# A hybrid attention and ConvFFN layer on one core: spreading the later attention steps over the blocks by a table

## Chip, core and metric

One core of one Trainium2 chip runs the whole layer in a single launch. Times are device microseconds (us) of that core. The engines are TensorE (PE, with its weight loads as PEld), VectorE (DVE), ScalarE (ACT), GpSimd (POOL) and SyncE (SP, which here only issues DMAs).

## What is computed

One layer on a sequence of 2048 tokens of width 1024, all in float32:

```
h = rms_norm(x);  sb_q, sb_k, sb_v, g_q, g_k, g_v, g_lr, g_og = split(h @ w_in)
o_sb  = head_rms_norm(stick_breaking_attention(q, k, v))     # 8 heads of 64, strictly causal
o_gla = head_rms_norm(gla_chunked(...)) * silu(g_og)         # 4 heads, gated linear attention
x = x + concat(o_sb, o_gla) @ w_out
h = rms_norm(x)
a, val = split(causal_depthwise_conv(h @ w_ffn_up), 2)       # 2 x 2816 columns, 3 taps
x = x + (silu(a) * val) @ w_ffn_down
return rms_norm(x)
```

In stick-breaking attention the weight of key s for query t is beta_ts times the product of (1 - beta_tj) over s < j < t, with beta the sigmoid of the scaled score.

## The kernel before

Every float32 factor is split into a high part in float32r and a low part that holds the rest, and a product is three matmuls (high by high, high by low, low by high). The split is one copy on ACT (line 102 for weights, line 94 for results in PSUM) and one subtraction on POOL or DVE (lines 103 and 95).

The sequence is cut into four blocks of 512 tokens. First come the input projections, the gated linear attention, the output gate, and the stick-breaking attention of block 0 (the first 675 us). Then `ffn(b)` runs for the four blocks in turn. Each call has an output projection with w_out (`accumulate`, two halves of 512 columns), a norm with transposing matmuls (tpu), and three groups of 8, 7 and 7 chunks of the FFN. A group is an up stage (`ups`, per chunk two pieces of 24 matmuls) and a down-projection (`accumulate` again, tiles d and draw). In block 0 the weights come raw from DRAM: SP loads a chunk (uraw, draw, or wraw for the first half of w_out), ACT and POOL split it, POOL's queue writes the split pair to DRAM scratch (wup, wdn, wou). Blocks 1 to 3 load the split pairs.

The attention of blocks 1, 2 and 3 stands beside this as a second generator, `attention_steps`, `later` in the driver. Its units are (block i, head h, key block c), four steps each: 288 steps and 8 more to drain the pipeline, 296 in all. Step n makes the weights of its query tile (z on PE, two sigmoids on ACT, a scan, cy and a product on DVE; in a diagonal unit, c equal to i, POOL masks two tiles), transposes those of step n - 5 (tp on PE, ws on ACT and DVE), and multiplies those of step n - 6 with v (acc on PE). z lies in a pool of two PSUM banks. A finished head is normed and written to osc, from which the next block's output projection reads.

PE's instructions stand in the order in which the program is written; the other engines' and the queues' order is made by a scheduler from it. The driver fixes PE's order: `ffn` yields the estimated length of what it has just issued (2.6 after each half of an up piece of 24 matmuls or a chunk of a down-projection; 395.2 a block), the driver adds that to `clock`, and issues attention steps until their number has caught up:

```
for dt in ffn(b, oT, order if b == 0 else None, nextT):
    clock += dt
    while done < total and done < clock / SPAN * total:
        next(later, None)
        done += 1
```

`LEAD` steps (4) are made before the first block. `need` is asserted: block b + 1 finds its attention done. While `done < total`, a down-projection gathers in the four banks that it shares with the up stage, and later in four of attention's banks, with six more buffers for its weights (`after_attention`).

Of the kernel before, what the change touches and what calls it, by code (L numbers as in the profile page):

```python
# [21 lines left out]
NB = S // TB  # L22
# [11 lines left out]

LAG = 5

SPAN = 1030.0
FILL = 4.0

FIRST = 4 * SBH + LAG + 4  # L40
# [10 lines left out]
def hybrid_block_kernel(ctx, tc, x, attn_norm_g, w_in, w_gate_up, b_gate_up, sb_out_g,  # L51
# [66 lines left out]
    if True:  # L118
# [21 lines left out]
        for n in (6, 7, 8, 9, 10, 11, 14, 15, 0, 1, 2, 3, 4, 5, 12, 13):  # L140
            b, u = n // 4, n % 2
# [319 lines left out]
    class Ring:  # L461
# [3 lines left out]
        def next(self):  # L465
            self.n += 1
            return self.items[(self.n - 1) % len(self.items)]
# [487 lines left out]
    total = 4 * SBH * (2 + 3 + 4) + LAG + 3  # L955
    need = [0, 4 * SBH * 2 + LAG + 3, 4 * SBH * 5 + LAG + 3, total]
    done = 0
    clock = 0.0
    results = []
    order = (4, 5, 6, 7, 0, 1, 2, 3)  # L960
    oT = [oT.get(f) for f in order]
# [2 lines left out]
        done += 1  # L964
    for b in range(NB):
        nextT = []
        for dt in ffn(b, oT, order if b == 0 else None, nextT):
            clock += dt
            while done < total and done < clock / SPAN * total:
                next(later, None)  # L970
                done += 1
        assert b + 1 == NB or done >= need[b + 1]
        oT = nextT
# [27 lines left out]
```

## Time and profile before

| | |
|---|---|
| median of 3 runs | 2754.53 us (2751.18 to 2754.88) |
| the profiled execution | 2760.47 us, its span 2758.8 us |
| PE, PEld busy (share of the span) | 2694.3 us (98%), 2234.3 us (81%) |
| DVE, ACT, POOL busy | 1685.5 us (61%), 1147.0 us (42%), 611.6 us (22%) |
| chain that ended last | PE 86%, DVE 5%, DMA 4%, ACT 2% |
| granted clock of PE, mean | 0.996 |

The first instruction of the profile is time 0. In the profiled execution block 0's `ffn` runs from about 678 to 1265 us, block 1's to 1830, block 2's to 2336 and block 3's to 2751. The last attention step stands in block 2's second up stage. A wait is named by what PE was about to do and by the instruction that released it. An engine's busy time counts an instruction from its start to its end; PE's matmuls overlap.

### The profile page before, as it was taken

The page shows a single profiled execution, that of the slowest core. Times are in us where ns is not written, and L with a number is a line of the kernel's source. Part 1 is how long each engine was busy: PE and PEld are TensorE (multiplying, and loading weights), DVE is VectorE, ACT ScalarE, POOL GpSimd, SP SyncE. Part 2 cuts the span into 40 slices and gives each one's busy share as a digit, 9 for nine tenths or more (in the row PEclk, how much of TensorE's full clock was granted, in tenths as well). Part 3 has the DMA queues.
Part 4 walks back from the last instruction along what each step waited for, and adds up shares of the span by engine and source line. Part 5 has one row for each costly group of instructions (what it writes and reads, how often), then busy time and mean ns, then how long its engine had stood idle before and what let it go on. Part 6 is the DMA issues. An engine that isn't in the chain of part 4 may idle for free.

```text
span 2758.8 us, 36075 instructions
## 1 busy us (share of the span) xinstructions
PE 2694.3 (98%) x13004; PEld 2234.3 (81%) x13004; DVE 1685.5 (61%) x2778; ACT 1147.0 (42%) x2371; POOL 611.6 (22%) x937
## 2 busy tenths in 40 slices
PE   8999999999799999999999999999999999999998
PEld 7878888888688778887888888888888888888887
DVE  5246755467677687876776777777867334242333
ACT  5455533345465455554543444445434222220112
POOL 2001212215555556542111111111110000000000
PEclk9999999999999999999999999999999999999999
DMA  6214644467667677768455555574554656555552
GB/s 191 92 64 173 228 144 156 131 188 242 224 225 257 224 243 255 243 236 274 156 185 181 175 174 174 186 253 152 177 177 150 231 192 221 203 197 191 198 191 84
DMA packets 232169, 526.92 MB, mean 191 GB/s; under 512 B 32294, under 2 KB 120630, under 8 KB 209462
## 3 DMA queue, kind: packets, MB, share of 16 engines
q1 hardware_dynamic: 200742, 387.76, 42.3%
q0 software_dynamic: 31104, 136.33, 13.9%
q8 instruction: 102, 1.67, 0.3%
q14 instruction: 77, 0.63, 0.1%
q10 hardware_dynamic: 144, 0.52, 0.1%
HBM read 382.99 MB, written 141.56 MB: 190 GB/s over the span
## 4 chain that ended last, share of the span: by engine, by line
PE 86%; DVE 5%; DMA 4%; ACT 2%; issue 1%; POOL 1%; SPq 0%; ACTq 0%; POOLq 0%; DVEq 0%
PE ups L886 11%; PE ups L887 11%; PE ups L888 11%; PE d L765 7%; PE d L764 7%; PE d L766 7%; PE z L533 4%; PE tp L566 4%; PE mm L170 2%; PE mm L168 2%; PE mm L169 2%; PE acc L582 2%; PE mm L180 2%; PE mm L179 2%; PE mm L178 2%; PE acc L581 2%
## 5 line engine op out<-in xcount | busy, mean ns | idle before, releaser
L886 PE MATMUL ups<-h2h,u 128*128 128x512 f32 x1408 | 552.2, 392 | 3.9 <-DVE x L791 3.9
L887 PE MATMUL ups<-h2l,u 128*128 128x512 f32 x1408 | 551.1, 391 | 0.0
L888 PE MATMUL ups<-h2h,u 128*128 128x512 f32 x1408 | 550.3, 391 | 0.0
L886 PEld LDWEIGHTS ups<-h2h,u 128*128 128x128 f32 x1408 | 265.2, 188 | 60.6 <-DVE x L791 4.3
L95 DVE TENSOR_TENSOR ws<-tp,ws 128x512 fp32r<-128x512 f32 (+1 forms) x320 | 194.0, 606 | 193.2 <-ACT ws L94 192.3
L888 PEld LDWEIGHTS ups<-h2h,u 128*128 128x128 f32 x1408 | 265.0, 188 | 57.2
L887 PEld LDWEIGHTS ups<-h2l,u 128*128 128x128 f32 x1408 | 265.0, 188 | 55.4
L764 PE MATMUL d<-d,g 128*128 128x512 f32 x736 | 290.4, 395 | 3.8 <-ACT d L102 1.3
L94 ACT ACTIVATE ws<-tp 128x512 fp32r<-128x512 f32 (+1 forms) x320 | 170.3, 532 | 297.0 <-PE tp L566 292.8
L765 PE MATMUL d<-d,g 128*128 128x512 f32 x736 | 288.7, 392 | 1.2 <-POOL d L103 1.2
L766 PE MATMUL d<-d,g 128*128 128x512 f32 x736 | 288.4, 392 | 0.0
L898 DVE SCALAR_TENSOR_TENSOR ct<-ups,cwb,ct 128x511 f32<-128x511 f32 x176 | 131.7, 748 | 249.4 <-POOL ct L897 196.2
L893 ACT ACTIVATE ct<-ups,cwb 128x512 f32<-128x512 f32 x176 | 136.5, 775 | 340.0 <-PE ups L888 339.8
L549 DVE TENSOR_TENSOR_SCAN wtB<-mt,cy 128x512 f32<-128x512 f32 x192 | 249.0, 1297 | 4.4 <-ACT mt L538 4.3
L791 DVE TENSOR_TENSOR x<-d,x 128x512 f32<-128x512 f32 x128 | 85.8, 683 | 164.1 <-PE d L766 164.0
L897 POOL TENSOR_TENSOR ct<-ct,hadd 128x2 f32<-128x2 f32 x132 | 26.7, 202 | 688.5 <-ACT halo L895 324.3
L538 ACT ACTIVATE mt<-z 128x512 f32<-128x512 f32 (+2 forms) x320 | 170.6, 533 | 14.3 <-PE z L536 6.2
L764 PEld LDWEIGHTS d<-d,g 128*128 128x128 f32 x736 | 138.3, 188 | 35.3 <-DVE x L791 2.8
L765 PEld LDWEIGHTS d<-d,g 128*128 128x128 f32 x736 | 138.3, 188 | 31.2 <-POOL d L103 1.8
L766 PEld LDWEIGHTS d<-d,g 128*128 128x128 f32 x736 | 138.2, 188 | 30.8
L168 PE MATMUL mm<-hh,w 128*128 128x512 f32 x384 | 151.3, 394 | 0.0
L170 PE MATMUL mm<-hh,w 128*128 128x512 f32 x384 | 149.3, 392 | 0.9 <-POOL w L103 0.9
(265 smaller groups left out, 5374.2 us busy)
## 6 DMA issues: line engine op xcount, KB each, us to landing
u<-wup SPq DMA_DIRECT2D x132, 1024.0 KB, 4.7
d<-wdn SPq DMA_DIRECT2D x94, 512.0 KB, 3.5
wup<-u POOLq DMA_DIRECT2D x44, 1024.0 KB, 6.6
kvA<-kvs POOLq DMA_DIRECT2D x52, 512.0 KB, 4.6
uraw<-in_w_ffn_up_dram SPq DMA_DIRECT2D x44, 512.0 KB, 4.7
wdn<-d POOLq DMA_DIRECT2D x44, 512.0 KB, 4.9
d<-wou SPq DMA_DIRECT2D x38, 512.0 KB, 4.6
dw<-wdn SPq DMA_DIRECT2D x38, 512.0 KB, 4.3
```

Source lines behind the costliest of these rows:

```text
L94: nc.scalar.activation(hi, ps, AF.Copy)
L95: nc.vector.tensor_tensor(out=lo, in0=ps, in1=hi.bitcast(F32), op=ALU.subtract)
L168: nc.tensor.matmul(ps, whi[k][:, fs], hh[b][k // 4][:, k % 4, :], start=(k == 0), stop=False)
L170: nc.tensor.matmul(ps, wlo[k][:, fs], hh[b][k // 4][:, k % 4, :], start=False, stop=(k == KT - 1))
L538: nc.scalar.activation(m[:, lo:TB], z[:, :width], AF.Sigmoid, scale=-0.125)
L549: nc.vector.tensor_tensor_scan(out=pp[:, ::-1], data0=mr, data1=mr, initial=1.0 if prev is None else prev, op0=ALU.mult, op1=ALU.bypass)
L764: nc.tensor.matmul(accs[t], gh[:, ts], whi, start=(ci == 0), stop=False)
L765: nc.tensor.matmul(accs[t], gh[:, ts], wlo, start=False, stop=False)
L766: nc.tensor.matmul(accs[t], gw[:, ts], whi, start=False, stop=(ci == G - 1))
L886: nc.tensor.matmul(ps, whi[:, k, :], hk, start=(k == 0), stop=False)
L887: nc.tensor.matmul(ps, whi[:, k, :], lk, start=False, stop=False)
L888: nc.tensor.matmul(ps, wlo[:, k, :], hk, start=False, stop=(k == KT - 1))
```

## The change

The one rate for all blocks becomes a table with a number for each block, and the count starts anew at each block: in block b, `RATE[b]` steps per 395 units of its own clock, on top of those made before it. SPAN gave 296 / 1030 * 395 = 113.5 a block from the first unit on, with the four steps ahead counted in it. The last block has no steps in either.

```diff
-SPAN = 1030.0
+
+DENSE = 395.0
+RATE = (86, 130, 113)
...
-    clock = 0.0
...
         nextT = []
+        clock, begun = 0.0, done
         for dt in ffn(b, oT, order if b == 0 else None, nextT):
             clock += dt
-            while done < total and done < clock / SPAN * total:
+            while b + 1 < NB and done < total and done < begun + clock / DENSE * RATE[b]:
                 next(later, None)
                 done += 1
```

No instruction is added or removed; the order differs from the first output projection on. Line numbers of the changed kernel are two higher from there on. Three places:

PE, the first half of block 0's output projection (d is its PSUM tile, wsplit and wmore its split weights, z the scores of a step, tp the transposes of an earlier step). Before, its first step:

```order
L764 MATMUL d_6374<-wsplit,g_0_5527 128x512
L765 MATMUL d_6374<-wsplit,g_0_5527 128x512
L766 MATMUL d_6374<-wsplit,g_1_5528 128x512
L647 MATMUL tpo<-ident,ohp 128x128 x4
L533 MATMUL z<-kvA,qA 128x512 x2
L764 MATMUL d_6371<-wmore,g_0_5976 128x512
```

With the change, its first two steps:

```order
L768 MATMUL d_6373<-wsplit,g_1_5528 128x512
L535 MATMUL z<-kvA,qA 128x512 x2
L766 MATMUL d_6371<-wsplit,g_0_5527 128x512
...
L768 MATMUL d_6374<-wsplit,g_1_5528 128x512
L568 MATMUL tp<-ident,wtA 128x128 x4
L535 MATMUL z<-kvA,qA 128x512 x2
L766 MATMUL d_6371<-wmore,g_0_5976 128x512
```

The first step stood behind 72 matmuls of the projection and now stands behind nine; the second, with the first transposes, stood twelve matmuls later and now comes behind 24 in all.

ACT at the same place (mt and wt are a step's sigmoids, u the third weight of the up stage, d and wsplit and wmore weights of the output projection). Before:

```order
L102 ACTIVATE d_6310<-draw 128x512
L102 ACTIVATE wsplit<-wraw 128x512 x2
L538 ACTIVATE mt_5034<-z 128x384
L540 ACTIVATE wtA<-z 128x384
L538 ACTIVATE mt_5035<-z 128x512
L540 ACTIVATE wtA<-z 128x512
L102 ACTIVATE wmore<-wraw 128x512
L102 ACTIVATE u_6308<-uraw 128x1024
L102 ACTIVATE wmore<-wraw 128x512
```

With the change:

```order
L104 ACTIVATE d_6310<-draw 128x512
L540 ACTIVATE mt_5034<-z 128x384
L542 ACTIVATE wtA<-z 128x384
L540 ACTIVATE mt_5035<-z 128x512
L542 ACTIVATE wtA<-z 128x512
L104 ACTIVATE u_6308<-uraw 128x1024
L104 ACTIVATE wsplit<-wraw 128x512
L540 ACTIVATE mt_5034<-z 128x512
L542 ACTIVATE wtB<-z 128x512
L104 ACTIVATE wsplit<-wraw 128x512
L96 ACTIVATE ws_5042<-tp 128x512
```

The split of the up weight moved ahead of both wsplit and of the first ws; it was behind wsplit and ahead of one wmore.

ACT, near the end of block 0's first down-projection (d are splits of its weight chunks, ws copies of a step's transposed weights). Before:

```order
L102 ACTIVATE d_6310<-draw 128x512
L94 ACTIVATE ws_5042<-tp 128x512
L538 ACTIVATE mt_5035<-z 128x256
L540 ACTIVATE wtB<-z 128x256
L102 ACTIVATE d_6309<-draw 128x512 x2
L94 ACTIVATE ws_5043<-tp 128x512
```

With the change:

```order
L104 ACTIVATE d_6309<-draw 128x512
L104 ACTIVATE d_6310<-draw 128x512
L104 ACTIVATE d_6309<-draw 128x512
L96 ACTIVATE ws_5042<-tp 128x512
L540 ACTIVATE mt_5035<-z 128x256
L542 ACTIVATE wtC<-z 128x256
```

Three splits stand in a row where two did, as fewer steps lie between them.

## Rows read from the trace of the kernel before

**Rows 1.** Windows: stretch, length; busy PE, PEld, DVE, ACT, POOL; clock, DMA, GB/s:

```profile
678.00:1265.00 587.00, 558.17 (x2704) 459.92 (x2702) 430.49 (x649) 309.97 (x622) 323.34 (x379) 0.99 0.71 243
1265.00:1830.00 565.00, 560.79 (x2758) 465.70 (x2759) 413.35 (x668) 252.46 (x535) 87.21 (x187) 1.00 0.55 185
...
2636.00:2712.00 76.00, 76.00 (x337) 62.94 (x336) 33.52 (x47) 18.36 (x26) 2.56 (x13) 1.00 0.46 160
1675.00:1778.00 103.00, 103.00 (x499) 85.49 (x498) 83.14 (x132) 49.61 (x104) 16.06 (x33) 1.00 0.50 171
```

**Rows 2.** Waits of PE, 675 to 1265 us: us in total, times, longest:

```profile
PE acc L582 <- DVE ws L95: 6.4, 7, 2.1
PE d L764 <- ACT wmore L102: 5.5, 1, 5.5
PE ups L886 <- DVE x L791: 3.9, 1, 3.9
PE d L765 <- POOL wmore L103: 3.3, 1, 3.3
PE tpu L856 <- DVE dg L851: 2.5, 1, 2.5
PE d L764 <- ACT d L102: 1.3, 1, 1.3
PE d L764 <- DVE x L791: 1.3, 2, 0.8
PE d L765 <- POOL d L103: 1.2, 2, 0.9
PE d L764 <- DVE ct L900: 1.2, 1, 1.2
PE acc L581 <- ACT ws L94: 1.1, 2, 0.9
PE d L765 <- POOL wsplit L103: 0.8, 1, 0.8
PE z L533 <- ACT wtA L540: 0.8, 1, 0.8
```

**Rows 3.** Waits of PE, 1265 to 1830 us, those of attention:

```profile
PE acc L581 <- ACT ws L94: 1.0, 1, 1.0
...
PE acc L582 <- DVE ws L95: 0.9, 2, 0.7
```

**Rows 4.** Windows of the three half-clock stretches after 675 us, columns as in rows 1:

```profile
706.49:710.76 4.27, 4.27 (x12) 3.18 (x10) 0.00 (x0) 0.00 (x0) 0.41 (x1) 0.50 0.98 393
946.90:949.89 2.99, 2.99 (x8) 2.31 (x7) 2.48 (x4) 0.00 (x0) 1.61 (x2) 0.50 0.99 390
1022.08:1025.07 2.99, 2.99 (x9) 2.34 (x8) 2.30 (x5) 0.90 (x3) 0.84 (x3) 0.50 0.94 224
```

**Rows 5.** Timeline, first output projection: start, length, engine, instruction [idle before <-releaser]:

```profile
677.78 0.40 PE L764 MATMUL d<-wsplit,g 128*128 128x512 f32 x1
...
681.56 4.47 SPq L880 DMA_DIRECT2D uraw<-in_w_ffn_up_dram  x2
...
687.48 0.49 ACT L540 ACTIVATE wtA<-z 128x384 f32<-128x384 f32 x1
...
694.91 0.68 DVE L555 TENSOR_TENSOR wtA<-wtA,wtB 128x512 f32<-128x512 f32 x1
...
700.21 1.06 ACT L102 ACTIVATE u<-uraw 128x1024 fp32r<-128x1024 f32 x1 [8.62 <-DMA uraw<-in_w_ffn_up_dram]
```

**Rows 6.** Timeline, end of the first down-projection, ACT and PE:

```profile
943.07 0.63 ACT L102 ACTIVATE d<-draw 128x512 fp32r<-128x512 f32 x1 [4.65 <-DMA draw<-in_w_ffn_down_dram]
...
945.56 0.50 PE L886 MATMUL ups<-h2h,u 128*128 128x512 f32 x1 [3.88 <-DVE x L791]
```

**Rows 7.** Tile cy, block 0 then block 1: duration in ns, min/median/max:

```profile
L553 DVE TENSOR_TENSOR cy<-wtB,mt x65: 129/159/2061, 685.4 to 1260.1; 128x1 f32<-128x1 f32 x65
...
L553 DVE TENSOR_TENSOR cy<-wtB,mt x81: 142/159/163, 1272.5 to 1827.1; 128x1 f32<-128x1 f32 x81
```

## Prediction

> **What bounds it now.** I read first the windows by block [rows 1]. TensorE (PE) has an instruction in flight for 558 of block 0's 587 us, 561 of block 1's 565 and all of two pure stretches, so PE sets the pace everywhere, and what can be won is what PE loses. The difference between the blocks is in the other columns: POOL works 323 us in block 0, which splits weights, and 87 us in block 1, which reads them split; DVE works about the same in both.
>
> The share of PE busy time hides how full PE is. The Trainium skill, Perfetto Trace Analysis, section Identifying the Most-Contended Engine, says that matmul busy time is no good measure of headroom and LDWEIGHTS busy share is; the page of the profile has 81% there, which by that rule alone would leave 19%, some 520 us (an estimate from that page's rule). The trace sets the scale: in the last up stage, with no attention and no gap in PE, weight loads fill 62.94 of 76 us, 82.8%, and in block 1 465.70 of 565, 82.4%; a full PE reads so here [rows 1]. Block 0 has 459.92 of 587, 78.3%. At 82.4% its loads would take 558 us: some 29 us are lost in block 0, and almost nothing in block 1.
>
> The waits of PE say where [rows 2]: twelve kinds, 29.3 us, in block 0. Four things are mixed there. (a) The start of the first output projection, 5.5 + 3.3 + 0.8 for its weights and 0.8 for a z bank, 10.4 us. (b) Attention's own chain, acc on ws, 6.4 + 1.1 = 7.5 us. (c) Banks that come free late in the down-projections (3.9, 1.3, 1.2), and splits that come late there or in the output projection's second half (1.3, 1.2), 8.9 us. (d) The rstd chain, 2.5 us. On top, PE runs at 0.50 of its clock, the lower level of 1.2 GHz, over 4.27 + 2.99 + 2.99 us behind idle stretches; half of that, 5.1 us, is lost [rows 4]. Block 1 has only 1.9 us of waits on ws in 114 steps [rows 3].
>
> **What the change moves.** By the code's own clock (395.2 units per block) the three blocks run 110, 114 and 68 steps now, after the four ahead; with the table they run 87, 131 and 74. So 23 steps leave block 0, 17 go to block 1 and 6 to block 2. No instruction is added or taken away.
>
> A step's price on PE: the third up stage of block 1 is 103 us long and holds 21 steps, the same stage without steps 76 us [rows 1]; (103 - 76) / 21 = 1.29 us. So 23 x 1.29 = 29.7 us leave block 0 and come back as 21.9 + 7.7 us later. Where PE is full this sums to zero. A step's DMA issues (a key/value load on POOL's queue per four steps, a query load per head) and its write of the head's result on SP's queue move with it; POOL's and SP's queues in block 0 lose about six key/value loads and two or three result writes, and no wait of rows 2 is on one of them. Their worth is taken as zero: POOL is busy 55% of that block. So the answer lies in the waits.
>
> **Attention's waits in block 0, (b)**: 7.5 us, and the half-clock stretch at 1022 us behind one of them, 1.5 us: 9.0. With 24% fewer steps proportion alone takes off 2.2; if only close-packed steps collide, all 9.0 go. A step may come after every half of an up piece (12 matmuls); the up stages of block 0 go from three steps in four such halves to about one in two, but the diagonal units still wait on POOL behind weight splits. I take half, **-4.5** (ends -9 and +2, the upper one for the seven collisions of rows 2 falling otherwise).
>
> **Down-projections, (c)**: 8.9 us and the stretch at 946.9 us, 1.5: 10.4. The largest item is a chain on ACT: the split of a weight chunk waits 4.65 us for its DMA, the ws copy and the sum into x stand behind it, and PE's next bank is released 3.88 us late [rows 6]. The order rows show three splits in a row ahead of ws where there were two, so that this block is not gone for sure. PE also has less attention to fill with, while each chunk takes its DMA, ACT and POOL as before. Half of the 5.4 there, and 1.8 of the other 5.0, which are DVE's and the splits' queues: **-4.5** (ends -10.4 and +4, one more such wait).
>
> **The first output projection, (a)** is worked through, since the table starts its count at the four steps already made: five steps fall into the projection's first half, where there were two. PE starts at 677.78 and meets the fifth step's z after nine matmuls, at 679.9 [rows 5]. The z pool has two banks; the third z's sigmoids end at 688.0 (687.48 + 0.49), a wait of 8.1. Fifteen matmuls of 0.23 (76 / 337 in the pure stretch of rows 1) follow to 691.4; then the transposes need the fourth weight tile, done at 695.6 (694.91 + 0.68): 4.2. A z pair and 24 matmuls, 26 x 0.23, lead to 701.6. Now acc needs ws, which on ACT stands behind the split of the third up weight, whose load was issued at 681.56 and starts at 700.21 [rows 5]. Its 1.06, five more ACT operations of about 0.5 and one of 0.7 on DVE (the sigmoid and the product of the same rows) end near 704.5: 2.9. The waits are 15.2 against 10.4, but two steps more are done by then, 2.6: **+2** (ends -4 and +8; the load's landing alone can move it by the 4.65 that rows 6 show for a late one).
>
> The rstd wait and block 1's waits on x and on its first transposes are untouched.
>
> **Block 1** gets runs of five or six steps in consecutive half-pieces, where it had three. DVE per half-piece: 33.52 / 28 = 1.20 of dense work, and (83.14 - 33.52) / 21 = 2.36 a step, 3.56 in all; PE takes 76 / 28 + 1.29 = 4.0 [rows 1]. DVE still has 11% left inside a run. Its 1.9 us of waits on ws [rows 3] would be 2.2 in proportion; I take **+1** (ends 0 and +14, see the third rival). Block 2 keeps its rate, 113 a block, and runs some 25 units longer: the down-projection there still finds attention in its first half and keeps the shared banks, as all of block 1's do, which show no wait on them: 0.
>
> **Sum**: -4.5 - 4.5 + 2 + 1 = -6. The profiled execution took 2760.47 us (span 2758.8), so 2754.5 in its own terms; the median of the three runs is 2754.53, 5.9 below it, so **2748.5**.
>
> **Rivals.** 1. The collisions go altogether. POOL's work slows DVE: cy, a one-column product of 159 ns, takes up to 2061 ns in block 0 and at most 163 ns in block 1 [rows 7]. The Trainium skill, SBUF — State Buffer, section Who interferes with whom, says that the port pair of GpSimd and DVE is an exclusive lock for operations with two SBUF inputs, the second one blocking fully; rows 7 agree. As a mechanism here: every step moved takes its DVE products away from POOL's splits, so (b) and (c) both go, -9 - 10.4 + 2 + 1 = -16: 2738. Against it: only seven of 110 steps wait on DVE's ws now, at three steps in four half-pieces, so distance is not what makes most of them. 2. The weight chain takes it back: PE in block 0 has less of its own to do per chunk, and waits for chunks instead. (c) stays whole and (a) costs 8 in place of 2, -4.5 + 8 + 1 = +4.5, or with (a) at 2 -1.5: 2753 to 2759, say 2755. For it: rows 6 and the ACT order. Against: (c) is seven waits in all of block 0, so that the chain does not bind most chunks. 3. Slower: DVE becomes the bound in block 1's up stages. They hold 75 steps (66 now). Each pair of up pieces ends with a burst of DVE products, and a run of six leaves it less room to drain. If one step in four waits 0.9 us on ws, as one of block 0's does on average (6.4 / 7), that is 17 us: -6 + 17 - 1 = +10: 2764.5. It decides where DVE's time per half-piece passes PE's 4.0 us, 0.44 above my 3.56. Against it: now the same stages have 81% on DVE and next to no waits. 4. The change does not do what it says: excluded by the order rows, but its effect may be nil: 2754.5.
>
> **Chances.** Forecast 0.46, rival 1 0.16, rival 2 0.17, rival 3 0.17, rival 4 0.04. About 0.2% (5.5 us) is what a measurement of this kernel can tell from no change, so below 2749.0 is faster. Of the forecast's 0.46 the part beyond it is 0.27, as its sum lies just past the bound: faster 0.27 + 0.16 = 0.43; same 0.19 + 0.14 + 0.04 = 0.37; slower 0.03 + 0.17 = 0.20. The range runs from rival 1's centre less a microsecond to rival 3's centre, 2737 to 2765, and leaves out about half of each, 0.17. The forecast's own range is 2741 to 2756.
>
> **What would show it.** Block 0 should be 29.7 + 8 us shorter, near 549 us; its waits on ws near 3 to 4 us; its first stretch should show PE waiting for z and tp instead of wmore. Block 1 should be near 588 us with under 4 us of waits on ws. The forecast is wrong if block 1's ws waits pass 8 us (rival 3), or if block 0's down-projections wait as long as now (rival 2).

## Result and profile after

The changed kernel is slower. Its median is 2778.78 us (2762.35 to 2781.75, 7 runs) against 2754.88 (2751.18 to 2759.22, 7 runs) of the kernel before, a ratio of 1.0069 with a 95% interval of 1.0052 to 1.0087. Run unedited twice more, each time beside its own runs of the kernel before, it gave 1.0057 [1.0037, 1.0076] and 1.0056 [1.0040, 1.0072]. The forecast of 2748.5 was a gain where there is a loss, and the median lies outside the range of 2737 to 2765.

The first profile is of the execution with the lowest of the seven times (2762.35 us). A profile of another execution of the same program, label again, is of 2780.96 us and nearer to the median, so most rows below are from that one. First the windows by block, columns as in [rows 1], of the changed kernel's first profile:

```profile
677.80:1235.50 557.70, 532.24 (x2541) 439.25 (x2540) 385.80 (x563) 276.52 (x556) 311.27 (x354) 0.98 0.74 251
1235.50:1826.30 590.80, 585.50 (x2904) 485.68 (x2902) 454.52 (x745) 281.00 (x595) 100.10 (x209) 1.00 0.54 182
1826.30:2338.90 512.60, 507.83 (x2431) 420.39 (x2429) 313.81 (x495) 189.09 (x394) 50.14 (x125) 1.00 0.56 190
```

and of again:

```profile
678.60:1251.40 572.80, 537.42 (x2542) 441.83 (x2540) 387.75 (x563) 276.14 (x556) 312.80 (x354) 0.97 0.72 244
1251.40:1842.10 590.70, 585.42 (x2901) 485.63 (x2900) 454.55 (x745) 281.15 (x594) 100.40 (x209) 1.00 0.55 182
1842.10:2355.90 513.80, 509.54 (x2432) 421.81 (x2430) 313.52 (x494) 189.14 (x393) 49.90 (x125) 1.00 0.56 190
```

Cut at the same places (the first d matmul of each block), the kernel before has 591.70, 566.30 and 501.50 us; its block 0:

```profile
677.80:1269.50 591.70, 560.52 (x2720) 461.92 (x2719) 434.65 (x657) 313.01 (x631) 325.94 (x385) 0.99 0.72 244
```

So block 0 is shorter, as was meant, by 18.9 us in again and by 34.0 in the first profile, where 29.7 us of steps have left it; blocks 1 and 2 grow by 24.4 and 12.3 us in again and by 24.5 and 11.1 in the first profile. Blocks 1 and 2 are alike in the two executions to 1.2 us; what differs most from one execution to the next is block 0.

The loss is not idle time alone. Over the whole execution PE is busy 2705.4 us in again and 2694.3 before, with the same 13004 matmuls, at a mean granted clock of 0.992 and 0.996. So 11.1 of the 20.5 us between the two spans are PE running longer, about what the clock gives (an estimate: 0.004 of 2779 us is 11 us), and 9.4 are idle time of PE.

The waits of PE in block 0 of again (675 to 1251.4 us: us in total, times, longest), to be read against [rows 2]:

```profile
PE acc L584 <- DVE ws L97: 7.3, 7, 3.0
PE acc L583 <- ACT ws L96: 6.4, 4, 3.2
PE z L535 <- ACT wtA L542: 6.3, 2, 5.6
PE tpu L858 <- DVE dg L853: 4.8, 2, 3.2
PE d L766 <- ACT d L104: 3.2, 2, 2.8
PE tpo L649 <- DMA kvB<-osc: 2.4, 1, 2.4
PE d L767 <- POOL d L105: 2.2, 3, 0.9
PE d L766 <- DVE x L793: 1.5, 2, 1.2
PE tp L568 <- DVE wtA L557: 1.1, 2, 0.8
```

With one more of 0.9 they make 36.1 us, in a block with 23 steps fewer. Before, it is 32.1 us to the same cut: the 29.3 of [rows 2], which end at 1265 us, and two waits between there and 1269.5:

```profile
PE tpo L647 <- DMA kvB<-osc: 1.5, 1, 1.5
PE tpo L647 <- ACT wtC L540: 1.3, 1, 1.3
```

The waits for wmore (5.5 and 3.3) and the 3.9 on the second up stage's first bank are gone, as the prediction had it; waits on ws have gone up from 7.5 to 13.7, z's from 0.8 to 6.3, the rstd chain's (dg) from 2.5 to 4.8.

To place this, block 0 is cut into its seven stages, the first being the output projection with the tpu stage behind it. Lengths are those of windows; the steps are the sigmoids of tile mt counted in the same windows; the last column adds 1.29 us to the difference for each step that left, so that it holds the waits and what PE loses at its lower clock. Counting the moved work by PE's matmul records instead (27 us for 162 of them in [rows 1]) moves single stages by up to 1.6 us and changes no sign.

| stage | before, us (steps) | again, us (steps) | difference | without the steps |
|---|---|---|---|---|
| projection, tpu | 85.3 (13) | 96.3 (14) | +11.0 | +9.7 |
| up 1 | 116.4 (24) | 108.2 (18) | -8.2 | -0.5 |
| down 1 | 66.1 (12) | 61.0 (9) | -5.1 | -1.2 |
| up 2 | 110.3 (21) | 95.6 (15) | -14.7 | -7.0 |
| down 2 | 52.4 (10) | 52.1 (8) | -0.3 | +2.3 |
| up 3 | 103.5 (21) | 102.4 (16) | -1.1 | +5.4 |
| down 3 | 57.7 (11) | 57.2 (9) | -0.5 | +2.1 |
| block 0 | 591.7 (112) | 572.8 (89) | -18.9 | +10.8 |

Two things went wrong. The first output projection is 10 us longer, and what the three stages after it gain (8.7 us together) the last three stages, which had only 3.9 us of waits before, lose again (9.8 us).

### The profile page after: what moved, and what is told of

Read it like the earlier page. It is cut to its first block, busy times and chain, and to the rows that moved or that the text cites. A ratio compares the mean times of both kernels' runs of the same rounds, so it can differ in the third digit from the quotient of the medians.

```text
span 2760.6 us, 36068 instructions
## 1 busy us (share of the span) xinstructions
PE 2697.8 (98%) x13004; PEld 2237.7 (81%) x13004; DVE 1690.7 (61%) x2778; ACT 1145.7 (42%) x2371; POOL 611.2 (22%) x937
## 4 chain that ended last, share of the span: by engine, by line
PE 88%; DVE 5%; DMA 3%; ACT 2%; issue 1%; POOL 1%; SPq 0%; ACTq 0%; POOLq 0%; DVEq 0%
PE ups L888 11%; PE ups L889 11%; PE ups L890 11%; PE d L766 7%; PE d L767 7%; PE d L768 7%; PE z L535 4%; PE tp L568 4%; PE mm L172 2%; PE mm L170 2%; PE mm L171 2%; PE acc L584 2%; PE mm L181 2%; PE mm L182 2%; PE mm L180 2%; PE acc L583 2%
## 5 line engine op out<-in xcount | busy, mean ns | idle before, releaser
L766 PE MATMUL d<-d,g 128*128 128x512 f32 x748 | 296.4, 396 | 2.2 <-DVE x L793 1.2
L767 PE MATMUL d<-d,g 128*128 128x512 f32 x748 | 294.6, 394 | 1.7 <-POOL d L105 1.7
L768 PE MATMUL d<-d,g 128*128 128x512 f32 x748 | 294.1, 393 | 0.0
L766 PEld LDWEIGHTS d<-d,g 128*128 128x128 f32 x748 | 141.3, 189 | 34.4 <-DVE x L793 2.6
L767 PEld LDWEIGHTS d<-d,g 128*128 128x128 f32 x748 | 141.5, 189 | 32.2 <-POOL d L105 2.3
L768 PEld LDWEIGHTS d<-d,g 128*128 128x128 f32 x748 | 141.3, 189 | 31.6
L170 PE MATMUL mm<-hh,w 128*128 128x512 f32 x384 | 151.2, 394 | 0.0
L171 PE MATMUL mm<-hl,w 128*128 128x512 f32 x384 | 150.2, 391 | 0.0
```

The lines of the kernel that those rows point to most:

```text
L170: nc.tensor.matmul(ps, whi[k][:, fs], hh[b][k // 4][:, k % 4, :], start=(k == 0), stop=False)
L171: nc.tensor.matmul(ps, whi[k][:, fs], hl[b][k // 4][:, k % 4, :], start=False, stop=False)
L766: nc.tensor.matmul(accs[t], gh[:, ts], whi, start=(ci == 0), stop=False)
L767: nc.tensor.matmul(accs[t], gh[:, ts], wlo, start=False, stop=False)
L768: nc.tensor.matmul(accs[t], gw[:, ts], whi, start=False, stop=(ci == G - 1))
```

## Experiments

The theories at the start: A, that the early start of block 0's count, the steps in the first output projection, is the loss; B, that it is block 1's denser steps; C, that block 0's weights come late because there is less attention to cover them. Four runs share one set of runs of the kernel before (2757.79 us, 29 runs).

**again**: the changed kernel, no edit.

> The changed kernel once more, nothing edited, for a profile of a typical run: the one profile that exists (2762.35 us) is the fastest of seven runs whose median is 2778.78 us. All theories: a median of 2775 to 2780 us. Theory A (the start of block 0, where five steps now come early): the trace of a run near 2778 us has 10 us or more of additional PE waits and half-clock time before 765 us. Theory B (block 1's denser steps): the additional time is in block 1, as waits of acc on ws. Theory C (block 0's weights come late because it has less attention to cover them): it is in block 0's down-projections and up stages after 765 us.

Measured 2775.19 us (2764.11 to 2780.96, 6 runs), ratio 1.0057 [1.0037, 1.0076]. The loss is there a second time.

**late_start**: block 0 counts from 0 in place of the four steps made, with a rate that ends at the same 91.

```diff
-RATE = (86, 130, 113)
+RATE = (90, 130, 113)
+START = (0, None, None, None)
...
-        clock, begun = 0.0, done
+        clock, begun = 0.0, done if START[b] is None else START[b]
```

> The table, but block 0 counts the four steps ahead in it, as before the change: 90 per 395 units from nothing, so its first own step comes at 17.6 units and no longer at the first yield. Block 0 still ends with 91 steps made, blocks 1 and 2 as in the change. Theory A: near or below the kernel before, 2745 to 2758 us. Theories B and C: 2772 to 2780 us, as the change.

Measured 2758.36 us (2750.04 to 2770.77, 12 runs), ratio 1.0004 [0.9988, 1.0020]. It is 0.4 us above theory A's range and far from that of B and C. Nearly all of the loss is gone, with block 0 as thin and block 1 as dense as in the changed kernel. Its windows by block:

```profile
677.20:1231.40 554.20, 530.08 (x2542) 436.18 (x2541) 385.74 (x563) 276.91 (x556) 303.62 (x354) 0.99 0.74 252
1231.40:1823.70 592.30, 587.01 (x2902) 486.80 (x2900) 454.65 (x745) 281.15 (x594) 100.07 (x209) 1.00 0.55 182
1823.70:2338.00 514.30, 509.48 (x2432) 421.79 (x2430) 313.99 (x495) 189.24 (x394) 51.03 (x125) 1.00 0.56 190
```

Block 0 is 37.5 us shorter than before, 7.8 more than its steps, close to what the prediction had (29.7 + 8). Projection and tpu take 77.2 us with 10 steps, up 3 takes 98.0 with 17. But blocks 1 and 2 take 26.0 and 12.8 us more, where 23 steps at 1.29 us are 29.7: 9.1 us above that price, and nothing is won.

**early_start**: the old spread (114, 228 and 296 made at the ends), counted from the four steps made.

```diff
-RATE = (86, 130, 113)
+RATE = (109.5, 113.5, 113.5)
```

> The old spread (114, 228, 296 steps made at the ends of blocks 0, 1 and 2) but with the early start alone: block 0 counts from the four steps made, 109.5 per 395 units. Theory A: 2770 to 2780 us, most of the loss of the change. Theories B and C: 2752 to 2758 us, as the kernel before.

Measured 2764.41 us (2757.48 to 2768.73, 12 runs), ratio 1.0022 [1.0010, 1.0034], between the two ranges, so that both are missed. The early start costs 6.6 us without the table too, but less than the 16.8 that separate again and late_start: it and the thin block do not simply add.

**dense1**: block 0 as before, block 1 at the rate of 130, the rest in block 2.

```diff
-RATE = (86, 130, 113)
+RATE = (113.45, 130, 113)
+START = (0, None, None, None)
...
```

> Block 0 as before the change (114 steps made at its end, old start), block 1 at the change's 130 per 395 units (245 made at its end), the rest in block 2. The dense block 1 alone. Theory B: 2765 to 2780 us, with 8 us or more of waits of acc on ws in block 1. Theories A and C: 2752 to 2760 us.

Measured 2761.31 us (2754.87 to 2771.66, 12 runs), ratio 1.0017 [1.0003, 1.0031], 1.3 us above the range of A and C and 3.7 below that of B: the dense block 1 costs a little, 0.5% or more is not there. A leads, B is small.

The next question is what the early steps do. In the trace of again (timeline of ACT, first output projection: start, length, engine, instruction, idle before it and its releaser) the split of the third up weight stands in the middle of the work that PE waits for; before, it stood behind wsplit (the order rows of the change) and began at 700.21 [rows 5]:

```profile
699.53 1.06 ACT L104 ACTIVATE u<-uraw 128x1024 fp32r<-128x1024 f32 x1 [10.85 <-DMA uraw<-in_w_ffn_up_dram]
700.49 0.61 ACT L104 ACTIVATE wsplit<-wraw 128x512 fp32r<-128x512 f32 x1
...
702.49 0.59 ACT L96 ACTIVATE ws<-tp 128x512 fp32r<-128x512 f32 x1
```

and PE in the same stretch. Its wait for a bank of z ends before that split, both waits on ws stand behind it:

```profile
686.44 1.22 PE L535 MATMUL z<-kvA,qA 128*128 128x512 f32 x2 [5.56 <-ACT wtA L542]
...
693.62 0.33 PE L568 MATMUL tp<-ident,wtA 128*128 128x128 f32 x1 [0.34 <-DVE wtA L557]
...
703.13 0.80 PE L583 MATMUL acc<-ws,kvA 128*128 128x512 f32 x1 [3.23 <-ACT ws L96]
...
706.96 0.80 PE L584 MATMUL acc<-ws,kvA 128*128 128x512 f32 x1 [3.04 <-DVE ws L97]
```

For 10.85 us ACT waits for a load that nobody needs before the up stage. The transposes that its ws copies at 702.49 were done at 694.0 (693.62 + 0.33), and it did not take them first. In the first profile of the same program the load came sooner, and the wait was half as long:

```profile
693.27 1.06 ACT L104 ACTIVATE u<-uraw 128x1024 fp32r<-128x1024 f32 x1 [5.49 <-DMA uraw<-in_w_ffn_up_dram]
```

**two_u** and **two_u_b**: the changed kernel, but with two tiles in the ring of up weights until chunk 3, so that the third split can't be issued before the up stage.

```diff
-    ur = Ring([w_tile([P, 2, KT, P], F32R, f"u{n}") for n in range(3)])
+    us = [w_tile([P, 2, KT, P], F32R, f"u{n}") for n in range(3)]
+    ur = Ring(us[:2])
...
+                if b == 0 and c == 3:
+                    ur.items.append(us[2])
```

> The changed kernel, with its attention steps where they are, but the ring of the third buffer for first-matmul weights starts with two tiles in block 0 and gets its third at chunk 3, so the copy and split of the third up weight no longer stands on ACT in the first output projection (in the changed kernel run again it waited there 10.85 us for its load, until 699.53). Theory A1 (ACT works in order: the wmore, mt, wt and wsplit work queued behind that copy is late, and the output projection waits for its parts): the waits of acc on ws near 703 and 707 (3.4 + 3.6 us) go, the projection shrinks from 77.5 us to about 68 to 70, and the time to 2760 to 2766 us (ratio 0.998 to 1.003 to the kernel before). Theory A2 (the early steps cost by themselves, through z's wait on wtA of 5.6 us, tp and the dg waits of the next stage; the load is beside the point): those waits stay, the time stays at 2770 to 2778.

Measured 2769.67 us (2764.12 to 2772.26, 6 runs), ratio 1.0058 [1.0044, 1.0071] to 2757.46 (29 runs) of the kernel before. The two waits behind the split are gone from its trace, but the ratio is still that of the changed kernel. The next two runs put both side by side, on another chip.

> The changed kernel as it is, a third time, to stand beside the three others of this call on the same chip. Both theories: 2765 to 2780 us, median about 2775 (ratio 1.004 to 1.008).

> The kernel two_u once more, beside the changed kernel: its profile had lost 10 us in the output projection (67.3 against 77.5 us) while its ratio of 1.0058 stood where the changed kernel's was. Theory A1 (ACT blocked behind the split of the third up weight is half of the loss or more): at least 5 us under again_b. Theory A2 (the early steps' own waits are the loss): within 4 us of again_b.

Measured, with 2758.68 us (22 runs) for the kernel before: again_b 2775.67 us (2769.72 to 2778.88, 6 runs), ratio 1.0056 [1.0040, 1.0072]; two_u_b 2766.27 us (2760.63 to 2776.53, 12 runs), ratio 1.0029 [1.0017, 1.0042]. The two results for one edit don't agree: from nothing to 9.4 us. The traces do: projection and tpu take 83.3 us in two_u_b against 92.6 in again_b, and 7.0 of the 9.3 come back in up 1 (115.3 against 108.3), where ACT now waits 3.4 and 1.4 us for loads of up weights and PE 2.8 us behind it; a further 4.2 and 4.4 us are won in down 2 and down 3. So ACT's blocked split is shown as the cause of those two acc waits, and it is worth about half of the loss at most (9.4 of 17.0 us). PE's waits on z and dg stay, and its waits on ws in block 0 now lie behind the projection, the 2.8 us in up 1 among them (two_u_b, block 0, columns as above):

```profile
PE z L535 <- ACT wtA L542: 6.4, 2, 5.6
PE tpu L859 <- DVE dg L854: 5.1, 2, 3.1
PE acc L583 <- ACT ws L96: 4.7, 4, 2.8
```

**late_two_u** and **before_two_u**: the same two tiles in late_start and in the kernel before.

> The kernel late_start with the same two tiles to begin with. Theory A1: the copy of the third up weight stands later on ACT in late_start already, but still in the first output projection; with it gone a few us more go, 2748 to 2755 us. Theory A2: nothing is left to gain there, 2756 to 2760, as late_start.

> The kernel before, with its old spread of steps, and the two tiles to begin with. Theory A1: its own waits in the first output projection that stand behind that copy (acc on ws, 5 to 9 us with the half-clock stretch at 706 to 711) go, 2746 to 2752 us. Theory A2: as before, within 3 us.

Measured 2759.56 us (2750.88 to 2767.93, 12 runs), 1.0013 [1.0000, 1.0026], and 2754.55 us (2750.77 to 2758.79, 11 runs), 0.9997 [0.9985, 1.0009]. Both expectations of A1 missed: there is no gain. A2's are met. In before_two_u the waits for wmore (5.5 + 3.3) went, and block 0 is 6.3 us shorter in the profiled execution (585.4 against 591.7), but over the runs nothing is left of it that can be measured.

**late_flat**: late_start with block 1 at the old rate; the steps that leave block 0 are made in block 2.

```diff
-RATE = (90, 130, 113)
+RATE = (90, 113.5, 113)
```

> The kernel late_start with block 1 at its old rate of steps (113.5), so that the steps that leave block 0 (91 made at its end) are made in block 2. Theory B1 (block 1's denser steps give back what the thinner block 0 gains): 2750 to 2755 us, ratio 0.996 to 0.999. Theory B2 (what block 0 gains comes back wherever the steps go, since PE itself has them to do and each block's beginning waits the same): 2757 to 2760, as late_start.

Measured 2758.89 us (2751.54 to 2764.84, 12 runs), 1.0010 [0.9995, 1.0025]: B2. Block 0 is 36.7 us shorter (555.0), block 2 is 36.0 longer (537.5), for the same 23 steps. What a thin block 0 gains returned in both places that were tried.

Two runs split the early steps in two.

**first_half**: the five steps of the projection's first half early, then none until the count of late_start catches up.

```diff
+            want = begun + clock / DENSE * (RATE + (0,))[b]
+            if b == 0:
+                want = max(min(want, 9), clock / DENSE * 90)
+            while b + 1 < NB and done < total and done < want:
```

> Only the five steps of the first half of the first output projection stand early, as in the changed kernel; then none is made until the count of late_start has caught up at the end of the projection, and from there it is late_start (91 made at block 0's end). Theory H1 (the early steps cost where they stand, in the projection's first half, through the waits on wtA, and by what they push back on ACT): 2768 to 2776, z's wait of about 5.6 us stays. Theory H2 (the cost is in the second half and the next stage, where wider steps meet the dg chain on DVE): 2755 to 2761, as late_start, and the tpu stage takes about 10 us, not 18.

**second_half**: the complement, one step there, then nine in the second half, and from its end the changed kernel's count.

```diff
+                want = clock / DENSE * 90 if clock < 20.8 else min(want, 4.7 + (clock - 20.7) * 0.4)
```

> The complement: one step in the first half of the first output projection, as in late_start, then nine in its second half, so that the count from its end on is the changed kernel's, step for step. H1: 2757 to 2763, the waits on wtA of 5.6 us go, the dense second half adds a few. H2: 2768 or more, the tpu stage stays at about 18 us.

Measured 2768.56 us (2765.68 to 2781.03, 8 runs), 1.0038 [1.0022, 1.0054], and 2768.41 us (2765.22 to 2773.74, 9 runs), 1.0032 [1.0019, 1.0045]. Neither theory has it alone: each half costs some 10 us, more than half of the loss. In first_half PE waits as again does,

```profile
683.57 1.22 PE L535 MATMUL z<-kvA,qA 128*128 128x512 f32 x2 [5.53 <-ACT wtA L542]
699.98 0.79 PE L583 MATMUL acc<-ws,kvA 128*128 128x512 f32 x1 [2.99 <-ACT ws L96]
703.81 0.80 PE L584 MATMUL acc<-ws,kvA 128*128 128x512 f32 x1 [3.04 <-DVE ws L97]
```

and its wait for dg is 0.4 us; in second_half none of these stands, and the dg wait is 6.8 us (675 to 770 us):

```profile
PE tpu L858 <- DVE dg L853: 6.8, 2, 6.0
```

The dg wait was still open. **two_u_hold**, **again_hold** and **before_hold** make no step from the last third of the projection's second half until tpu is issued, in two_u, the changed kernel and before_two_u (there with 10 and 0.4 for 12 and 0.3).

```diff
+            want = begun + clock / DENSE * (RATE + (0,))[b]
+            if b == 0 and clock > 35:
+                want = 12 if clock < 52.8 else min(want, 12 + (clock - 52.6) * 0.3)
+            while b + 1 < NB and done < total and done < want:
```

> The kernel two_u, but no step is made from the last third of the first output projection's second half until all of the tpu stage is issued (the count stands at 12; the steps left out follow in the first up stage). Theory D (the half of the loss that two_u leaves is the dg chain on DVE behind wide attention work, 5.1 us of dg waits and a tpu stage of 18 us): tpu stage near 10 to 11 us, time 5 to 7 us under two_u, 2759 to 2762 (ratio 1.000 to 1.002). Theory P (what is left comes from where the later steps of block 0 fall against the chunks, whatever stands beside tpu): within 3 us of two_u, 2764 to 2770, since the catch-up in the up stage returns it.

> The changed kernel with the same hold and nothing else. D: 2768 to 2771 (5 to 7 us under the changed kernel's 2775). P: 2772 to 2778.

> The kernel before with the two tiles to begin with and the same hold (count 10, then catching up), its spread otherwise. D: its own dg wait of 2.65 us goes as well: 2749 to 2753, ratio 0.997 to 0.999. P: as before_two_u, within 3 us (ratio 0.9985 to 1.001).

Measured, with 2758.07 us (17 runs) for the kernel before: 2773.54 us (2770.10 to 2775.91, 5 runs), 1.0058 [1.0040, 1.0077]; 2778.96 us (2775.48 to 2781.47, 4 runs), 1.0079 [1.0060, 1.0098]; 2757.68 us (2754.88 to 2766.15, 12 runs), 1.0001 [0.9990, 1.0013]. Theory D's numbers are missed in all three, but the test is not clean. The dg waits shrink only to 3.1 us, since the rstd chain waits for ACT and POOL as well, and the steps held back cost more where they are caught up: waits on ws in block 0 are 15.0 us in two_u_hold (9.0 in two_u) and 19.4 in again_hold (13.7 in again). P's ranges are missed too, by 3.5 us in two_u_hold and 1.0 in again_hold, from the other side; only before_hold is where P put it. No version tried beats the kernel before by more than can be measured.

## Why the prediction was wrong

**What leaves and comes back** was right. 23 steps left block 0, 17 and 6 came to blocks 1 and 2 (112, 114 and 60 steps to 89, 131 and 66 by the sigmoids of mt), and nothing was added.

**Step (a), the first output projection, is the first that failed: "+2 (ends -4 and +8; the load's landing alone can move it by the 4.65 ...)".** With the tpu stage behind it, it was worth +9.7 in again, +6.0 in again_b and +0.2 in the first profile. The places and their order were right: z, tp, then acc on ws behind the split of the third up weight. In sum these waits were even shorter than forecast, 13.6 us for 15.2 (z 6.3, with 5.6 in the place of the 8.1; tp 1.1 for 4.2; acc 3.2 + 3.0 for 2.9, as DVE's ws came late a second time). What failed is the sum around them. The windows of the whole stage, before and in again, columns as in [rows 1]:

```profile
677.80:763.10 85.30, 69.60 (x344) 56.60 (x343) 55.34 (x78) 37.55 (x78) 48.55 (x64) 0.94 0.66 236
678.60:774.90 96.30, 75.26 (x345) 61.06 (x343) 56.67 (x80) 37.77 (x79) 47.35 (x65) 0.88 0.58 209
```

It put three things at nothing. First, the clock: with nearly the same matmuls PE is busy 75.3 us in place of 69.6, at a granted clock of 0.88 in place of 0.94. So of the 11.0 us only 5.3 are idle time, and 5.7 are PE at its lower level of 1.2 GHz. The clock of again is at or near 0.50 around 687, 703 to 710, 744 to 751 and 763 to 768 us, each time behind a wait of 2.8 us or more; before, it is in one place, around 702 to 711. Second, the rest of the stage. ACT's split of a weight comes 2.8 us late in the projection's second half (1.3 before), and the rstd chain, "untouched" in the prediction, takes 4.8 us in place of 2.5. The steps that now stand beside that chain are wide (full 512 columns where late_start has 128 and 256); without any there, in two_u_hold, 3.1 us are left of two_u's 5.0. second_half, with only this part, still loses 9.7 us. Third, the credit of 2.6 us for two steps done early: at the end of the stage 14 steps are done in place of 13, with the same matmuls, so nothing of it is left.

**Steps (b) and (c), "-4.5" each, held only as far as the second up stage.** Up 1 to up 2 give -8.7, about the -9 of the two. The waits named there did go: 3.9 on x at 945 us, 1.2 on ct, and of 5.0 us on ws between up 1 and up 2 (763 to 1022 us) 2.6 are left (768 to 1000 us in again). The failed part is the assumption that the other stages would stay as they were. From there to the end of the block, before had one wait of 1.1 on ws and 2.8 of others; again has 4.9 us on ws and 5.6 of others, with a fifth fewer steps. One cause is shown on DVE, in up 3 (groups of instructions: line, operation, tiles, count | busy us, mean ns). Of again:

```profile
L909 DVE TENSOR_TENSOR ct<-sg,ct 128x512 f32<-128x512 f32 x7 | 7.6, 1091 | 1.4 <-ACT sg L908 1.3
L913 DVE TENSOR_TENSOR g<-ct,g 128x512 fp32r<-128x512 f32 x6 | 6.4, 1062 | 0.9 <-ACT g L912 0.7
...
L557 DVE TENSOR_TENSOR wtA<-wtA,wtB 128x512 f32<-128x512 f32 x5 | 5.7, 1132 | 0.2
```

and of late_start, the same instructions:

```profile
L910 DVE TENSOR_TENSOR ct<-sg,ct 128x512 f32<-128x512 f32 x7 | 4.8, 688 | 2.8 <-ACT sg L909 2.7
...
L914 DVE TENSOR_TENSOR g<-ct,g 128x512 fp32r<-128x512 f32 x6 | 4.1, 686 | 0.7 <-ACT g L913 0.7
L558 DVE TENSOR_TENSOR wtA<-wtA,wtB 128x512 f32<-128x512 f32 x5 | 3.4, 687 | 0.3
```

In before, with 21 steps in this stage, the three means are 678, 691 and 684 ns. Those of again hide three single products of 2.9 us in place of 0.69; each begins just after one of POOL's weight subtractions has begun and ends just after it. A cy of 2.19 us, in place of 0.16, does the same (timelines of DVE and of POOL, again):

```profile
1099.81 2.19 DVE L555 TENSOR_TENSOR cy<-wtB,mt 128x1 f32<-128x1 f32 x1
...
1131.11 2.89 DVE L913 TENSOR_TENSOR g<-ct,g 128x512 fp32r<-128x512 f32 x1
...
1138.19 2.92 DVE L557 TENSOR_TENSOR wtA<-wtA,wtB 128x512 f32<-128x512 f32 x1
...
1151.09 2.90 DVE L909 TENSOR_TENSOR ct<-sg,ct 128x512 f32<-128x512 f32 x1
```

```profile
1099.53 2.46 POOL L105 TENSOR_TENSOR u<-uraw,u 128x1024 fp32r<-128x1024 f32 x1
...
1130.57 2.88 POOL L105 TENSOR_TENSOR u<-uraw,u 128x1024 fp32r<-128x1024 f32 x1 [3.23 <-ACT u L104]
...
1138.17 2.40 POOL L105 TENSOR_TENSOR u<-uraw,u 128x1024 fp32r<-128x1024 f32 x1 [1.31 <-ACT u L104]
...
1150.94 2.50 POOL L105 TENSOR_TENSOR u<-uraw,u 128x1024 fp32r<-128x1024 f32 x1 [1.15 <-ACT u L104]
```

The three are 6.6 us of DVE (three times 2.2) in a stage which late_start, with one step more, runs in 98.0 us against 102.4. PE waits 3.4 us in this stage, for 0.4 in late_start and 1.1 before. Two of its waits on ws stand behind slowed products, the first behind the cy and the second behind the product at 1131.11 (timeline of PE, again):

```profile
1103.78 0.50 PE L584 MATMUL acc<-ws,kvA 128*128 128x512 f32 x1 [1.04 <-DVE ws L97]
...
1135.69 0.33 PE L584 MATMUL acc<-ws,kvA 128*128 128x128 f32 x1 [0.95 <-DVE ws L97]
```

So some 2.0 of the 5.4 us of up 3 are seen to come from these meetings; behind the products at 1138 and 1151 us PE does not wait, and no run takes the meetings away by themselves. The Trainium skill, SBUF — State Buffer, section Who interferes with whom, says that a DVE instruction with two inputs in SBUF contends with a GpSimd instruction that reads SBUF, and that the port pair they share is an exclusive lock; these rows agree, and this is the rule that rival 1 used to forecast a gain. Fewer steps did not mean fewer such meetings in this stage: where the steps fall against the splits makes the difference, and the changed kernel moved them.

**Blocks 1 and 2, "+1" and "0"**: +2.5 and +4.6 (24.4 less 21.9, 12.3 less 7.7). Rival 3's place was wrong: block 1 has only 1.6 us of waits from its first up stage to its end (1315 to 1838 us). The loss is at the beginnings of the blocks, in the projection and the tpu stage: 79.5 us for 73.0 in block 1, with three steps more, and 77.6 for 71.7 in block 2, with none. Block 2's largest wait there (again, 1838 to 1910 us) is the rstd chain once more, beside 1.4 and 1.3 us on DVE's g and ws:

```profile
PE tpu L858 <- DVE dg L853: 2.2, 1, 2.2
```

The six steps that block 2 received are those of the prediction (66 for 60), so this loss is not theirs; late_start grows there by the same, 12.8 us.

With +2.7 before the first block and in block 3, the terms measured are 9.7 + 1.1 (10.8 - 9.7) + 2.5 + 4.6 + 2.7 = 20.6 us, where the spans differ by 2779.3 - 2758.8 = 20.5; the prediction had -6. Of its signs, block 0 near 549 us was 572.8, and waits on ws near 3 to 4 us were 13.7. Block 1 near 588 us was 590.7, with 3.3 us of waits on ws, so that rival 3's sign stayed away. Rival 2's "(a) costs 8 in place of 2" came nearest, but at 2755 it left out the later stages. Two slips in the sums changed little: 23 of 110 steps are 21%, not 24%, and the 8 in "29.7 + 8" is 7 by the terms (a) to (c).

What stays open is the half of the loss that two_u leaves. It goes when block 0's count starts late (late_start), and the rows place it in the projection, in tpu and in the last three stages; which of them weighs most was not settled, and the one edit aimed at tpu paid more elsewhere than it won.

## What to carry to other kernels

Work interleaved by a table is priced by where each piece falls on the in-order engines it shares, not by how many pieces a stage holds: a change of density moves every piece, also in stages that have no waits now, so count these as unknown, on the losing side too. Price a wait with what follows it: here PE's time at the lower clock behind its waits was as large as the added waits themselves. Ask of each copy that starts with a load what stands behind it on its engine, and take the load's landing from a spread of runs, not from one trace. A gain that comes from taking work out of one block is only a gain if the block that receives it has the room, stage by stage, its beginning included.

## What the hardware showed unexpectedly

The same load of the same program took 11.7 us from issue to landing in one execution and 17.1 in another (the first uraw load after 681 us, in the changed kernel's first profile, then in again):

```profile
uraw<-in_w_ffn_up_dram SPq DMA_DIRECT2D x1, 512.0 KB, 11.7
```

```profile
uraw<-in_w_ffn_up_dram SPq DMA_DIRECT2D x1, 512.0 KB, 17.1
```

In the two the queues move 403 and 407 GB/s between 681 and 700 us, and the next such load takes 15.9 and 16.6 us, so the sum of the traffic does not tell the executions apart; what does is not shown.

A product on DVE of two tiles in SBUF that begins while POOL subtracts is held until POOL is done: 2.89 to 2.92 us in place of 0.69, in three of the 18 products above. DVE's ws at 1147.85 us, one of whose inputs is in PSUM, takes its usual 0.68 us in the middle of a subtraction that runs from 1146.51 to 1148.92.
